# Keeping the high parts of weights in emitted order on ScalarE, in the mixing part of a two-block fp32 model

## The chip, the cores and the metric

The kernel runs on one core of a Trainium2 chip. The metric is the device time of one execution in microseconds (us); the kernel before takes 1950.87 us as the median of three runs, which lie between 1950.57 and 1951.28 us.

## The reference

A sequence of 256 tokens of width 1024 passes through two blocks. The first block has two layers, each with a half-weighted SwiGLU feed-forward, a mixing part, a cross-attention to 256 memory tokens and a second feed-forward. The second block (mLSTM, differential attention, a mixture of 32 experts) is left out here; the change does not reach into it. The mixing part projects the normed tokens to 3328 columns, gives half of the width to an RWKV-7 recurrence and half to a causal attention (MoBA), and projects both back:

```
h = rms_norm(x); p = h @ w_mix_in
# RWKV-7, 8 heads of 64, decay w, rates a, from p through small low-rank products
p = p + (token_shift(p) - p) * mu
state = state * w_t + (state @ -kk_t) b_t^T + v_t k_t^T        # one step per token
y_t = state @ r_t ; y = group_norm(y) + bonus ; y = y * gate
# MoBA: softmax(q k^T + bias) v within one block of 256 tokens, 8 heads
x = x + concat(y, moba) @ w_mix_out
k, v = split(mem @ w_kv)                                       # for the cross-attention that follows
```

All of it is float32.

## The kernel before

**Weights.** All dense weights are a stream of tiles of 128x1024 fp32 in a fixed order. `load` starts the DMA of the next one into a buffer named raw. `parts` (L541) splits one into a high part, `wh`, with an ACTIVATE of ScalarE (a copy rounded to fp32r), and a low part, `wl`, which is raw less wh, with a TENSOR_TENSOR of VectorE. The tokens are split in the same way into XH and XL. A product is then three matmuls (`mm3`): XH with wh, XH with wl, XL with wh. One tile takes 12 matmuls of 128x512. `prefetch` calls `parts` ahead of need, as far as buffers go: in the mixing part there are four raw buffers and two each of wh and wl (`RING`), so the wh of a tile can start only once TensorE is done with the tile two before it. In the feed-forwards other buffers are lent to this ring.

**The mixing part.** `mix` (L884) runs the projections one after the other (`proj`) and starts tasks beside them: `shifted` (token shift), `lora` (the small products), `rwkv_early` for two groups of heads (decays by scans on VectorE, sums that pass through GpSimd), `rwkv_late` with `rwkv_solve` (a 16x16 solve by many small VectorE instructions on a tile W, whose result comes back by DMA into the tiles c and is spread into Y) and `rwkv_chunk` (two chunks of 128 tokens), `moba`, and `xattn_k` (keys and values of the memory for the cross-attention). At its end `add_proj` multiplies by the output weights, which needs all of them.

**What sets the order.** The kernel's own `Weave` chooses which task emits next, by priorities and by a cost model (`Clock`) that says what is due. That gives the order in which instructions are emitted. A scheduler behind it then orders the instructions of each engine anew by when its own model holds them ready; the engine executes them in that order, one behind the other, and waits at the first that is not ready. `tc.keep_in_program_order(z)` adds to z an edge from the instruction emitted just before z on the same engine: z cannot be put ahead of that one. Instructions emitted earlier still may be put behind z.

Every instruction passes through one helper (`TimedEngine`), so all rows of the trace have its line, L378, and are told apart by the names of their tiles. In rows of the order the names carry numbers; the last number of a tile counts emissions.

Of the kernel before, what the change touches and what calls it, by code (L numbers as in the profile page):

```python
# [9 lines left out]
F32 = mybir.dt.float32  # L10
# [3 lines left out]
AF = mybir.ActivationFunctionType  # L14
# [19 lines left out]
class Cols:  # L34


    def __init__(self, *items):
        self.at, self.n = {}, 0
        for name, w in items:
            self.at[name] = (self.n, w)  # L40
            self.n += w
# [46 lines left out]
def stream():  # L88

    out = collections.deque()  # L90

    def put(name, *js):
        out.extend((name, j, i) for j in js for i in range(2))

    ada = iter([("ada", j, i) for j in range(24) for i in range(2)])

    def ffn(name):
        for c in range(NCH):
            for j in range(6):
                if j < 4:  # L100
                    out.append((name, 3 * c + j // 2, j % 2))
                elif c:
                    out.append((name, 3 * c - 1, j % 2))
                if c and (j == 3 or c % 5 == 0 and j == 4):
                    out.append(next(ada))
        put(name, 3 * NCH - 1)

    for l in range(2):
        ffn(f"ffn1{l}")
        put(f"mix{l}", *range(13))  # L110
        put(f"kv{l}", *range(4))
        put(f"mo{l}", *range(4))
        put(f"kv{l}", *range(4, 8))
        put(f"xq{l}", *range(4))
        put(f"xo{l}", *range(4))
        ffn(f"ffn2{l}")
    put("win", *range(14), 14, 15, 16, 17, 18, 19, 20, 21)
    put("br", *range(4))
    put("wo", *range(4))
    for e in range(32):  # L120
        put("exp", 3 * e, 3 * e + 1)
        if e:
            put("exp", 3 * e - 1)
    put("exp", 95)
    return out
# [126 lines left out]
class Clock:  # L252
# [18 lines left out]
    @staticmethod  # L271
    def span(ap):

        (step, parts), *dims = [(int(s), int(n)) for s, n in ap.ap]
        n = math.prod(z for _, z in dims)
        dims = sorted((z for z in dims if z[1] > 1 and z[0]), reverse=True)
        runs, size = [int(ap.offset) % step if step else int(ap.offset)], 1
        while dims and dims[-1][0] <= size:
            s, z = dims.pop()
            size += s * (z - 1)  # L280
        while dims:
            s, z = dims.pop()
            if len(runs) * z > 16:
                size += s * (z - 1)
            else:
                runs = [r + s * i for r in runs for i in range(z)]
        return ap.tensor.name, [(r, r + size) for r in runs], n, parts
# [160 lines left out]
class Prog:  # L448
    def __init__(self, ctx, tc, a):
        self.clock = Clock()  # L450
        self.tc, self.nc, self.a = tc, Timed(tc.nc, self.clock), a
        nc = self.nc
        pool = lambda name, **k: ctx.enter_context(tc.tile_pool(name=name, **k))
        self.cp = pool("cst", bufs=1)
        self.wp = pool("wts", bufs=2)
        self.ap_ = pool("act", bufs=2)
        self.pp = pool("psum", bufs=2, space=PSUM)
        self.dp = pool("dram", bufs=1, space=DRAM)
        self.uid = 0
        self.turn = {}  # L460
        self.weave = Weave(self.clock)
        self.spawn = self.weave.add
        self.order, self.loads, self.ahead = stream(), collections.deque(), collections.deque()
        self.chunks, self.mod = collections.deque(), None
        self.version, self.uses = [1, 1], 0
        self.sp, self.spare = None, {}
        self.behind, self.stop = [], None
        self.loan = {}
        self.tail = self.scaled = None

# [70 lines left out]
    def parts(self, raw):  # L541
        h, l = self.wtile("wh", F32R), self.wtile("wl", F32R)
        with ExitStack() as later:
            for z in self.behind:
                later.enter_context(self.tc.issue_after(z.ins))
            quiet, self.clock.quiet = self.clock.quiet, True
            self.nc.scalar.activation(h, raw, AF.Copy)
            self.nc.vector.tensor_sub(l, raw, h.bitcast(F32))
            self.clock.quiet = quiet
        return h, l  # L550

# [797 lines left out]
    def softmax(self, *parts):  # L1349

        nc = self.nc
        cut = lambda z, n, m: z[:, :n * m].rearrange("p (h k) -> p h k", h=n)
        mx, sm, out = [], [], []
        for dst, src, n, m in parts:
            mx.append(self.k("s8", 8))
            nc.vector.tensor_reduce(mx[-1][:, :n], cut(src, n, m), axis=AX.X, op=OP.max)
            nc.vector.tensor_scalar(mx[-1][:, :n], mx[-1][:, :n], -1.0, None, op0=OP.mult)
        yield 0, -0.5
        for (dst, src, n, m), z in zip(parts, mx):
            v, d = cut(src, n, m), cut(dst, n, m)  # L1360
            sm.append(self.k("s8", 8))
            for h in range(n):
                nc.scalar.activation(d[:, h], v[:, h], AF.Exp, bias=z[:, h:h + 1], accum_out=sm[-1][:, h:h + 1])
            out.append(d)
        yield 0, -0.3
        for (dst, src, n, m), z, d in zip(parts, sm, out):
            ri = self.k("s8", 8)
            nc.vector.reciprocal(ri[:, :n], z[:, :n])
            for h in range(n):
                nc.scalar.activation(d[:, h], d[:, h], AF.Copy, scale=ri[:, h:h + 1])  # L1370
        yield 0, self.due(*out)
        return out
# [1008 lines left out]
    def beyond(self, state, out):  # L2381
# [13 lines left out]
        with self.tc.If(most > P):  # L2395
# [10 lines left out]
            for e in range(8):  # L2406
# [21 lines left out]
             raw=2, wh=2, wl=2)  # L2428


def body(tc, a, out, stage=99):
    with ExitStack() as ctx:
        p = Prog(ctx, tc, a)
        w = p.weave

        def first():
            X = p.next_x(p.vec("gf10"))
            for n in range(min(stage, 8)):
                l, part = divmod(n, 4)
                norm = n == 7 and stage >= 9 and p.spawn(p.final_norm(), 1)  # L2440
                Z = None if n == 7 else p.next_x(p.vec(("gmx", "gxa", "gf2", "gf1")[part] + str((n + 1) // 4)))
                if part == 1:
                    kv = yield from p.mix(l, X)
                elif part == 2:
                    yield from p.xattn(l, X, kv)
                else:

                    p.lend({k: v for k, v in LOAN.items() if n < 7 or k != "raw"})
                    yield from p.ffn(f"ffn{part // 2 + 1}{l}", X)
                    p.lend({})  # L2450
                X = Z
                if norm:
                    yield norm

        with p.work(BUFS):
            p.setup()
            p.spawn(p.setup_later(), 5)
            w.finish(w.add(first(), 10))
            if stage == 9:
                p.settle()  # L2460
        if stage >= 10:
            p.sp = ctx.enter_context(tc.tile_pool(name="second", bufs=1))
            p.spare = SPARE
            with p.work(BUFS2):
                MX = w.finish(w.add(p.block2(), 10))
        if stage >= 11:
            with p.work(BUFS3):
                p.beyond(w.finish(w.add(p.moe(MX, out), 10)), out)
        else:
            for t in range(2):  # L2470
                tc.nc.sync.dma_start(out[t * P:(t + 1) * P], p.x[t])
# [18 lines left out]
```

## Time and profile before

| | us |
|---|---|
| median of three runs | 1950.87 |
| the profiled execution | 1949.61 |
| its span | 1947.6 |
| TensorE (PE) busy | 1897.4 (97%) |
| VectorE (DVE) busy | 1403.1 (72%) |
| ScalarE (ACT) busy | 1059.3 (54%) |
| GpSimd (POOL) busy | 73.3 (4%) |

PE is busy for 97% of the span and idle for 50 us. Of these, 18 us lie in the two mixing parts, one per layer, at 202 to 420 us and, with the same pattern, at 898 to 1116 us; 1.5 us lie in the 478 us between them, and 25 us after them. The mean granted clock over the span is 0.991 of full speed.

### The profile page before, as it was taken

To read this page: it belongs to the slowest core of one execution; us is meant where nothing else is said; L and a number is where in the kernel's file an instruction comes from. 1 tells how busy PE (TensorE), PEld (TensorE's weight loads), DVE (VectorE), ACT (ScalarE), POOL (GpSimd) and SP (SyncE) were. 2 spreads that over 40 slices of the span, in tenths; PEclk is the share of its full clock that TensorE was granted. 3 is DMA by queue.
4 is the path that set the end of the run, shared out by engine and by line. 5 is a ranking of instruction groups with operands and counts; after the bars stand their busy time and mean duration, and the time that the engine had idled before them with its cause. 6 is when DMAs were issued, how large, how long until landed. Compare 5 with 4: busy or idle time off the path is not lost.

```text
span 1947.6 us, 26262 instructions
## 1 busy us (share of the span) xinstructions
PE 1897.4 (97%) x9534; PEld 1532.9 (79%) x9534; DVE 1403.1 (72%) x2287; ACT 1059.3 (54%) x1606; POOL 73.3 (4%) x69
## 2 busy tenths in 40 slices
PE   8999999999999999999999999999999999999997
PEld 6888778888888878888787888888777786877775
DVE  6666787664666676666877655666687677999897
ACT  4444653655544444445536655444555546777674
POOL 0000011000000000000110000000001000000000
PEclk9999999999999999999999999999999999999999
DMA  8766432244566656665314253666564453999996
GB/s 280 249 223 226 128 126 68 86 155 159 172 211 222 216 205 215 220 213 173 134 41 127 97 189 117 222 221 215 183 202 139 150 182 139 337 340 360 332 337 223
DMA packets 114806, 381.41 MB, mean 196 GB/s; under 512 B 17080, under 2 KB 21864, under 8 KB 114544
## 3 DMA queue, kind: packets, MB, share of 16 engines
q1 hardware_dynamic: 114672, 379.68, 58.3%
q8 instruction: 77, 1.26, 0.3%
q14 instruction: 57, 0.47, 0.1%
HBM read 378.03 MB, written 3.17 MB: 196 GB/s over the span
## 4 chain that ended last, share of the span: by engine, by line
PE 76%; issue 11%; DVE 7%; ACT 2%; POOL 1%; DMA 1%; SPq 0%; DVEq 0%; POOLq 0%; ACTq 0%
PE mm L378 40%; PE acc L378 31%; PE tr L378 6%; DVE wl L378 3%; ACT wh L378 1%; POOL rs L378 1%; DVE el L378 1%; DVE s L378 1%; DMA raw<-in_w_dram 1%; DVE XL L378 0%; DVE t1k L378 0%; DVE AR L378 0%; DMA K<-in_mem_dram 0%; DMA x<-in_x_dram 0%; ACT s L378 0%
## 5 line engine op out<-in xcount | busy, mean ns | idle before, releaser
L378 DVE TENSOR_TENSOR wl<-raw,wh 128x1024 fp32r<-128x1024 f32 x648 | 785.2, 1223 | 320.2 <-ACT wh L378 317.2
L378 ACT ACTIVATE wh<-raw 128x1024 fp32r<-128x1024 f32 x648 | 676.3, 1057 | 522.6 <-PE mm L378 295.3
L378 PE MATMUL mm<-wh,XH 128*128 128x512 f32 (+1 forms) x1456 | 579.6, 400 | 3.0 <-ACT s L378 2.4
L378 PE MATMUL mm<-wl,XH 128*128 128x512 f32 (+1 forms) x1456 | 573.5, 394 | 2.6 <-DVE wl L378 2.1
L378 PE MATMUL mm<-wh,XL 128*128 128x512 f32 (+1 forms) x1456 | 571.3, 393 | 0.3
L378 PEld LDWEIGHTS mm<-wl,XH 128*128 128x128 f32 x1456 | 274.4, 188 | 65.7 <-DVE wl L378 10.7
L378 PEld LDWEIGHTS mm<-wh,XH 128*128 128x128 f32 x1456 | 274.7, 189 | 63.5 <-ACT s L378 3.8
L378 PEld LDWEIGHTS mm<-wh,XL 128*128 128x128 f32 x1456 | 274.2, 188 | 57.9 <-DVE XL L378 1.1
L378 PE MATMUL acc<-wh,X 128*128 128x512 f32 x352 | 143.0, 406 | 0.0
L378 PE MATMUL acc<-wh,T 128*128 128x512 f32 x352 | 139.1, 395 | 0.0
L378 PE MATMUL acc<-wl,X 128*128 128x512 f32 x352 | 139.1, 395 | 0.0
L378 PE MATMUL acc<-wl,XH 128*128 128x512 f32 x288 | 115.0, 399 | 2.9 <-DVE wl L378 2.7
L378 PE MATMUL acc<-wh,XH 128*128 128x512 f32 x288 | 114.5, 404 | 0.9 <-ACT XH L378 0.5
L378 PE MATMUL acc<-wh,XL 128*128 128x512 f32 x288 | 114.0, 396 | 0.0
L378 PE MATMUL acc<-wh,ah 128*128 128x512 f32 x256 | 85.7, 396 | 1.3 <-ACT ah L378 1.3
L378 DVE SCALAR_TENSOR_TENSOR el<-raw,vecs,el 128x512 f32<-128x512 f32 x84 | 63.1, 751 | 32.9 <-DMA raw<-in_w_dram 31.1
L378 PEld LDWEIGHTS acc<-wh,T 128*128 128x128 f32 x352 | 66.3, 188 | 15.9
L378 PEld LDWEIGHTS acc<-wl,X 128*128 128x128 f32 x352 | 66.4, 189 | 13.8
L378 PEld LDWEIGHTS acc<-wh,X 128*128 128x128 f32 x352 | 66.3, 188 | 13.4
L378 POOL TENSOR_TENSOR rs<-s,emh 128x2 f32<-128x2 f32 (+2 forms) x28 | 31.6, 1133 | 1147.3 <-DVE s L378 1144.7
L378 PEld LDWEIGHTS acc<-wl,XH 128*128 128x128 f32 x288 | 54.7, 190 | 18.3 <-DVE wl L378 7.5
L378 PEld LDWEIGHTS acc<-wh,XH 128*128 128x128 f32 x288 | 54.4, 190 | 12.5 <-ACT XH L378 1.2
(377 smaller groups left out, 2060.5 us busy)
## 6 DMA issues: line engine op xcount, KB each, us to landing
raw<-in_w_dram SPq DMA_DIRECT2D x696, 512.0 KB
ext<-ext SPq DMA_DIRECT2D x1, 2048.0 KB
K<-in_mem_dram SPq DMA_DIRECT2D x8, 256.0 KB
x<-in_x_dram SPq DMA_DIRECT2D x4, 256.0 KB
bi<-ext SPq DMA_DIRECT2D x4, 256.0 KB
sm<-ext SPq DMA_DIRECT2D x4, 256.0 KB
w<-gates SPq DMA_DIRECT2D x2, 512.0 KB
out_dram<-x SPq DMA_DIRECT2D x4, 256.0 KB
```

The costliest lines, as they stand in the source:

```text
L378: r = f(*args, **kw)
```

## The change

`Prog` gets a flag, `pinned`. It is True while `mix` runs. While it is, `parts` calls `keep_in_program_order` for the ACTIVATE that makes wh; the TENSOR_TENSOR that makes wl is not marked. This holds for every tile split in that time, whichever task asks for it. Nothing is added to or taken from the instructions of any engine.

```diff
@@ Prog.__init__
+        self.pinned = False
@@ Prog.parts
-            self.nc.scalar.activation(h, raw, AF.Copy)
-            self.nc.vector.tensor_sub(l, raw, h.bitcast(F32))
+            made = (self.nc.scalar.activation(h, raw, AF.Copy), self.nc.vector.tensor_sub(l, raw, h.bitcast(F32)))
+            for z in made[:1] if self.pinned else ():
+                self.tc.keep_in_program_order(z)
@@ body, first()
                 if part == 1:
+                    p.pinned = True
                     kv = yield from p.mix(l, X)
+                    p.pinned = False
```

The scheduler's order differs in both mixing parts in the same way. In each layer 17 of about 42 wh come behind work of ScalarE that they preceded, and what depends on them moves on VectorE and TensorE.

The first place is ScalarE in the second group's `rwkv_early` of the first layer, 264 to 290 us in the trace before. t1k, el and COPY t1k are steps of the decay; wh_2485 is the high part of the last tile of MoBA's query projection, wh_2546 that of the first tile of its key projection.

```order
-L378 ACTIVATE wh_2485<-raw_2374 128x1024
-L378 ACTIVATE wh_2546<-raw_2422 128x1024
-L378 ACTIVATE s_596_2604<-mm_2372,rh_1875 128x512
 L378 ACTIVATE t1k_2465<-acc_2459,half_1916 128x256
 L378 ACTIVATE t1k_2469<-acc_2459,half_1916 128x256
@@ -191,15 +186,17 @@
 L378 COPY t1k_2473<-s_561_2456 128x256
 L378 COPY t1k_2475<-s_561_2456 128x256
+L378 ACTIVATE wh_2485<-raw_2374 128x1024
 L378 ACTIVATE t1k_2520<-acc_2460,half_1916 128x256
 L378 ACTIVATE t1k_2528<-acc_2460,half_1916 128x256
```

wh_2485 went from ahead of t1k to behind COPY t1k (with four ACTIVATEs of el in between, which did not move), and wh_2546 further back.

The second place is VectorE at the same time. Y is filled from c, which a DMA brings from the solve; el_2503 is the first scan of the decay (its result is read by COPY pe and AR).

```order
 L378 COPY start<-el_2448 128x8
+L378 TENSOR_TENSOR Y_2221<-c_504_2237,csts 128x512
+L378 MEMSET el_2448 128x8
 L378 COPY pe_2533<-el_2503 128x4
 L378 TENSOR_TENSOR AR_2535<-rkv_1981,el_2503 128x2x128
-L378 MEMSET el_2448 128x8
-L378 COPY pe_2533<-el_2503 128x4
+L378 TENSOR_TENSOR wl_2486<-raw_2374,wh_2485 128x1024
+L378 TENSOR_TENSOR Y_2253<-c_513_2269,csts 128x512
 L378 SCALAR_TENSOR_TENSOR el_2504<-el_2448,start 128x512
```

wl_2486, which stood in the middle of the solve's instructions on W, now stands behind the first Y, which came later, and behind AR.

The third place is ScalarE at the start of the output projection, 400 to 413 us. XH there is the high part of what is multiplied, K keys on their way through TensorE's transposes, wh_3931 a tile of the output weights.

```order
-L378 ACTIVATE wh_3931<-raw_3834 128x1024
 L378 ACTIVATE XH_2150<-t1k_3902 128x2x128
 L378 ACTIVATE K_3893<-tr_3907 128x512
+L378 ACTIVATE XH_2150<-t1k_3916 128x2x128
 L378 ACTIVATE K_3894<-tr_3921 128x512
-L378 ACTIVATE XH_2150<-t1k_3916 128x2x128
+L378 ACTIVATE wh_3931<-raw_3834 128x1024
 L378 ACTIVATE wh_3949<-raw_3873 128x1024
```

wh_3931 went from ahead of two XH and two K to behind all four; its wl on VectorE moved behind the XL in the same way.

## Rows read from the trace of the kernel before

**Rows 1.** Busy time of each engine over the span, from the page.

```profile
PE 1897.4 (97%) x9534; PEld 1532.9 (79%) x9534; DVE 1403.1 (72%) x2287; ACT 1059.3 (54%) x1606; POOL 73.3 (4%) x69
```

**Rows 2.** Groups by line: busy us, mean ns; idle us before, its releaser.

```profile
L378 DVE TENSOR_TENSOR wl<-raw,wh 128x1024 fp32r<-128x1024 f32 x648 | 785.2, 1223 | 320.2 <-ACT wh L378 317.2
L378 ACT ACTIVATE wh<-raw 128x1024 fp32r<-128x1024 f32 x648 | 676.3, 1057 | 522.6 <-PE mm L378 295.3
```

**Rows 3.** Windows: stretch, length, busy of PE, PEld, DVE, ACT, POOL, clock, DMA, GB/s.

```profile
202.00:420.00 218.00, 209.25 (x1396) 171.51 (x1394) 159.01 (x360) 123.21 (x246) 25.07 (x22) 0.98 0.34 106
898.00:1116.00 218.00, 208.65 (x1391) 170.84 (x1390) 158.06 (x354) 122.78 (x246) 24.98 (x22) 0.98 0.32 101
420.00:898.00 478.00, 476.48 (x2167) 388.47 (x2166) 311.28 (x392) 230.18 (x307) 2.09 (x3) 1.00 0.62 204
```

**Rows 4.** Waits, 202 to 420 us: who waits for whom, sum, times, longest.

```profile
ACT wh L378 <- PE mm L378: 22.6, 15, 4.6
```

**Rows 5.** Timeline, first group's rwkv_early: start, us, instruction, idle before it.

```profile
234.76 0.71 ACT L378 COPY t1k<-s 128x256 f32<-128x256 f32 x2 [0.52 <-POOL s L378]
235.87 0.47 PE L378 MATMUL mm<-wh,XH 128*128 128x512 f32 x1
236.17 1.23 DVE L378 TENSOR_TENSOR_SCAN el<-el,start 128x512 f32<-128x512 f32 x1
245.68 1.06 ACT L378 ACTIVATE wh<-raw 128x1024 fp32r<-128x1024 f32 x1 [4.63 <-PE mm L378]
249.56 0.30 PE L378 MATMUL tr<-csts,rkv 128*128 128x128 f32 x1 [1.51 <-DVE rkv L378]
```

**Rows 6.** Timeline, second group's rwkv_early and first solve.

```profile
268.91 2.73 POOL L378 TENSOR_TENSOR s<-s,emh 128x8 f32<-128x8 f32 x1 [20.97 <-DVE s L378]
272.22 1.06 ACT L378 ACTIVATE wh<-raw 128x1024 fp32r<-128x1024 f32 x1 [4.00 <-PE mm L378]
274.17 0.83 ACT L378 ACTIVATE t1k<-acc,half 128x256 f32<-128x256 f32 x2
275.14 0.20 DVE L378 TENSOR_TENSOR W<-W,t1k 32x28 f32<-32x28 f32 x1
276.48 0.70 ACT L378 COPY t1k<-s 128x256 f32<-128x256 f32 x2
276.93 0.74 PE L378 MATMUL tr<-csts,t1k 128*128 128x128 f32 x4 [0.67 <-ACT t1k L378]
277.51 1.27 POOL L378 TENSOR_TENSOR t1k<-csts,pe 128x256 f32<-128x256 f32 x2 [5.87 <-DMA c<-W]
278.22 0.84 DVE L378 TENSOR_TENSOR AR<-rkv,el 128x256 f32<-128x256 f32 x1
278.55 0.50 PE L378 MATMUL mm<-wh,XH 128*128 128x512 f32 x1 [0.88 <-ACT s L378]
280.32 0.67 DVE L378 TENSOR_TENSOR Y<-c,csts 128x512 f32<-128x512 f32 x1
283.24 1.97 PE L378 MATMUL tr<-csts,Y 128*128 128x128 f32 x8 [1.64 <-DVE el L378]
285.04 2.62 PE L378 MATMUL acc<-X,A 128*128 128x128 f32 x16
```

**Rows 7.** Windows in the same stretch.

```profile
279.50:280.00 0.50, 0.50 (x3) 0.40 (x2) 0.50 (x1) 0.00 (x0) 0.00 (x0) 0.50 0.00 0
286.50:287.00 0.50, 0.50 (x7) 0.50 (x6) 0.19 (x1) 0.19 (x1) 0.00 (x0) 1.00 0.64 205
```

**Rows 8.** Timeline, preparation of the memory beside the second chunk.

```profile
352.29 0.59 ACT L378 ACTIVATE T<-acc 128x512 f32<-128x512 f32 x1
353.16 1.00 DVE L378 TENSOR_REDUCE s<-bi 128x2 f32<-128x256 f32 x2
```

**Rows 9.** Timeline, start of the output projection.

```profile
409.92 0.42 ACT L378 ACTIVATE XH<-t1k 128x256 fp32r<-128x256 f32 x1 [0.49 <-DVE t1k L378]
410.26 0.39 PE L378 MATMUL mm<-wh,XH 128*128 128x512 f32 x1
```

**Rows 10.** Timeline, two further idle times of TensorE in the mixing part.

```profile
327.47 0.44 PE L378 MATMUL tr<-csts,YL 128*128 128x128 f32 x2 [1.02 <-DVE YL L378]
346.26 0.63 PE L378 MATMUL tr<-csts,K 128*128 128x128 f32 x4 [0.72 <-DMA K<-in_mem_dram]
```

## The prediction

> **What bounds the kernel now.** The page's busy times come first: PE is busy for 97% of the span, DVE for 72%, ACT for 54% [rows 1]. So TensorE bounds the whole, and a change of order on ACT shows in the time only where it makes PE idle, ends an idle time of PE, or changes the clock that PE is granted. The windows say how much there is to win where the change acts: in the first mixing part PE is busy for 209.25 of 218 us, in the second for 208.65; it idles 8.75 and 9.35 us, against 1.5 us in the 478 us between [rows 3]. The groups show the pair that the change moves: making wh takes 1.06 us, making wl 1.22 us, and before wl DVE has idled 317 us in all for wh [rows 2]. A wh that comes late is thus followed by a wl that comes late, 2.3 us from the start of one to the end of the other. The waits show the other side: in the first mixing part ACT stood with a wh at its head until PE let go of the buffer, 15 times, 22.6 us in all, longest 4.6 us [rows 4]. In that time the ACT work queued behind wh waited as well. The change turns this around: the wh that are moved wait behind ACT work, instead of ACT work behind them. For each place the question is which of the two PE meets first.
>
> PE needs 0.22 us for a matmul (478 us by 2167 in the stretch without gaps [rows 3]), so 2.65 us for the 12 of one tile. Since the same instructions run before and after, I count for each place the idle time of PE that appears less that which goes.
>
> **The change part by part.** Per layer 17 wh move. Most have room: between the end of such a wh and the first matmul on it lay 1.8 to 7.9 us, by my reading of the timeline, and the ACT work put ahead of it is shorter. These cost nothing, as long as PE has the tile before, 2.65 us of work, as cover; a wh without that cover costs up to the 2.3 us above. Four places are left.
>
> *First group's rwkv_early (228 to 250 us).* wh moves behind nine short ACT instructions, of which the last, COPY t1k, waited for POOL and ended at 235.47 [rows 5]. So wh ends at 236.5. Its wl on DVE moves behind the scan that ended at 237.40 [rows 5], and comes to 238.2 with some 0.4 us off for the chain that starts earlier. PE used this tile from 235.87 [rows 5] and can go on with wh alone for two matmuls: about 1.65 us idle, and 0.5 more because the transposes behind it come at a worse moment, +2.1. In return the wait of 1.51 us at 249.56 goes: it was for DVE, which had waited for ACT work behind the wh that stood 4.63 us at ACT's head [rows 5]; a gap of 0.4 us goes as well. Sum 0, from -1.5 (only the gain) to +2 (only the loss).
>
> *Second group's rwkv_early and first solve (264 to 290 us).* Before, the wh at 272.22 stood 4.00 us at ACT's head, t1k came behind it at 274.17, COPY t1k at 276.48, and PE waited 0.67, 0.88 and 1.64 us for this chain: 3.19 us [rows 6]. After, the chain goes ahead. Its COPY waits only for POOL, which ended at 268.91 + 2.73 = 271.64 [rows 6]; I take 271.4, since DVE feeds POOL a little earlier. COPY then ends at 272.1 and wh at 273.2. PE does two matmuls on it, until 273.65, and needs wl. On DVE wl now stands behind the first Y, and Y needs c from the solve's DMA. The solve's last instruction on W ended at 275.34, with two wl of 1.22 us standing in its chain; without them, about 273.5 (some of the room goes to other work). From W's end to c's arrival, which POOL waited for, went 277.51 - 275.34 = 2.17 us [rows 6]. So c is back at 275.7, Y (0.67), two small copies and AR (0.84) follow, and wl runs from 277.2 to 278.4: PE idles 278.4 - 273.65 = 4.75 us. Later the chain acc<-X,A to acc<-Y,T, which had the tile's matmuls beside it, comes earlier (near 283.2, not 285.04 [rows 6]) and with a single matmul between; the copy T between them takes 0.59 us [rows 8], about 0.85 with the hand-overs. Sum 4.75 + 0.85 - 3.19 = +2.4. Bounds: -3.2 if wl is not held (all three waits gone), +5 if Y comes as late as before, since the first Y at 280.32 would put wl two to three us later.
>
> *Memory preparation beside the second chunk (340 to 363 us).* Two wh move behind XH, s, X and T, the last ending at 352.88, and the first wl behind reductions that ended at 354.16 [rows 8]. PE runs the chunk's chain alone, 1.2 us short of wl at its end, and about 0.7 us short at T, where eight matmuls, 1.8 us, lay beside the chain: +1.9. Bounds: 0 (the chunk's end comes earlier by as much) to +3.4 (1.8 of cover gone, and 1.6 for wl).
>
> *Start of the output projection (400 to 413 us).* wh moves behind two XH and two K, its wl behind both XL. The second XH ended at 410.34 [rows 9]; with no wl ahead of its source on DVE it comes about 0.9 us sooner, the K behind it ends at 410.0, wh at 411.05, wl at 412.3. PE was ready for the tile at 410.26 [rows 9]: 0.8 us idle for wh, two matmuls, 0.85 us for wl: +1.65, from 0 to +1.7.
>
> *Absorbed.* Two waits of PE of 1.02 and 0.72 us end with DVE or a DMA [rows 10]. If PE comes later there, these shrink: -0.7, from -1.7 to 0.
>
> *The clock.* From 279.5 to past 286 us PE had a granted clock of 0.50, its lower level of 1.2 GHz, and 1.00 again at 286.5; before the fall stood the waits of 0.67 and 0.88 us, inside it that of 1.64 [rows 6, 7]. My sum supposes one such stretch per layer after, too: its cost is in both times and drops out.
>
> The Trainium skill (TensorE: Matmul & The Clock Gate, HAM oscillation — how this bites in real kernels) says that pauses of TensorE between bursts of matmuls put it back to the lower clock. The trace agrees in that the fall came behind a group of waits, though the pauses here were each under 1 us; by that rule the stall of 4.75 us would bring a fall too, which changes nothing here, and each further stall might, which is the third rival.
>
> **Sum.** 0 + 2.4 + 1.9 + 1.65 - 0.7 = +5.25 us per layer, and both layers move alike: +10.5. The profiled execution took 1949.61 us, its span 1947.6; 1949.61 + 10.5 = 1960.1. It lies 1.26 us below the median of the runs, 1950.87, so the median after is 1961.4; I say 1961. The bounds add up to -6.4 and +12.1 per layer, about -13 and +24 in all.
>
> **The rivals.**
> *Faster: the early chains pay.* The wh at 272.22 and 245.68 no longer stand at ACT's head, and what PE waited for behind them comes early [rows 5, 6]. If c is back by 274 us, wl is not held by Y; then -3.2 and -1.5 at the first two places, and half of the loss at the others, +1.8: -2.9 per layer, 1950.87 - 5.8 = 1945. It decides if PE's wait for the wl behind Y is under 2 us. For it: 22.6 us of such waits of ACT [rows 4]. Against: W's chain and 2.17 us of DMA don't leave room for it.
> *No change.* The edge binds wh to one instruction only, most wh have room, and what is late at one place is taken from PE's idle time at the next, of which there are 8.75 us [rows 3]: 1951. Against: the waits of [rows 10] can take 1.7 us, not 6.
> *Slower still: a second stretch at the lower clock.* If the stalls at 340 to 363 us bring one of 6.8 us more, as 279.5 to 286.3, PE does half of that in it: +3.4 per layer, (5.25 + 3.4) x 2 = 17.3, 1968. For it: a fall behind waits as short as these [rows 6, 7]. Against: the waits of [rows 10] lie at such places too, and the mean clock of the mixing part, 0.98, leaves room for just the one stretch.
>
> **How the numbers follow.** Forecast 0.45, faster 0.24, no change 0.18, slower still 0.13. Within 0.2%, 3.9 us, counts as no change, since that is about what a measurement of this kernel can tell. So faster 0.24, same 0.18, slower 0.58. The range must leave out no more than 0.2: from 1945, which cuts off half of the faster case, to 1969, which holds the third rival but for its tail. The likeliest case by itself has 1955 to 1966.
>
> **What would show it right or wrong.** Right: in the second group's rwkv_early, a wait of PE for wl of 4 to 5 us near 274, in place of those of 0.67, 0.88 and 1.64; on DVE wl directly behind AR; acc<-X,A about 2 us earlier; at the output projection two waits of 0.8 us for wh and wl; PE's idle time in the mixing part near 14 us instead of 8.75. Wrong: c's DMA back before 274.5, so that the wait is under 2 us; a wait of 1.5 us still at 249.56; a second stretch at 0.50, or none, in the clock; or a difference that lies outside the two mixing parts, where I count nothing.

## The result and the profile after

The changed kernel takes 1961.68 us (median of five, 1959.52 to 1965.16), the kernel before on the same chip 1950.57 (1948.84 to 1951.28). The ratio is 1.0056, 95% interval 1.0044 to 1.0069: slower by 8.6 to 13.5 us. The forecast was 1961.

The page of the kernel after: TensorE is busy for 2 us more than before [rows 1] in a span 11.9 us longer, so most of what was added is idle time. Between wl and wh, and between wh and PE, the idle times shift as a change of order would have it [rows 2]: VectorE waits longer for wh, ScalarE less for PE.

```profile
PE 1899.4 (97%) x9534; PEld 1528.9 (78%) x9534; DVE 1404.3 (72%) x2287; ACT 1058.5 (54%) x1606; POOL 70.8 (4%) x69
```

```profile
L378 DVE TENSOR_TENSOR wl<-raw,wh 128x1024 fp32r<-128x1024 f32 x648 | 785.0, 1223 | 334.7 <-ACT wh L378 333.2
L378 ACT ACTIVATE wh<-raw 128x1024 fp32r<-128x1024 f32 x648 | 676.1, 1057 | 507.1 <-PE mm L378 279.6
```

The windows of the two mixing parts, cut at the same points of the work as in [rows 3], and the stretch between them. PE idles 12.98 and 12.26 us in place of 8.75 and 9.35; 478 us between the parts have 1.55 us idle, as before. The forecast had near 14 us of idle time in a part.

```profile
202.69:426.16 223.47, 210.49 (x1396) 170.45 (x1395) 159.30 (x360) 122.91 (x246) 23.57 (x22) 0.98 0.33 103
904.36:1126.43 222.07, 209.81 (x1391) 169.52 (x1390) 157.98 (x354) 122.46 (x246) 23.95 (x22) 0.98 0.31 99
427.00:905.00 478.00, 476.45 (x2165) 388.32 (x2165) 311.34 (x393) 229.20 (x304) 2.09 (x3) 1.00 0.62 203
```

The waits of 202 to 427 us. ACT's wait with a wh at its head [rows 4] went from 22.6 us in 15 times to 14.1 in 8, and PE's wait for wl, 0.2 us before, is now the largest of PE's.

```profile
ACT wh L378 <- PE mm L378: 14.1, 8, 4.3
PE mm L378 <- DVE wl L378: 4.6, 7, 2.2
PE mm L378 <- ACT wh L378: 1.1, 3, 0.4
```

**Lag.** To see where time is lost, the matmuls of two executions are taken each in its own order and compared at the points at which the same amount of work is done (each form weighted with its usual time from one start to the next, 0.227 us for 128x512). The difference in time there is the lag behind before. Differences of the lag are what a stretch costs. Where two executions run their matmuls in different orders the lag depends on the weights: at 264, 300, 962 and 998 us by up to 0.5 us in most runs, in e5, e9 and e11 by up to 2, and in e9 and e11 by up to 1 at 340, 400, 1034 and 1098; at the ends of the mixing parts it does not. In us, at times of the kernel before:

| run | 202 | 264 | 300 | 340 | 400 | 420 | 898 | 962 | 998 | 1034 | 1098 | 1118 |
|---|---|---|---|---|---|---|---|---|---|---|---|---|
| after | 0.7 | 0.9 | 3.1 | 4.2 | 5.1 | 6.2 | 6.4 | 5.9 | 7.9 | 8.4 | 9.4 | 10.4 |
| e1 early tiles only | 0.0 | 0.0 | 1.6 | 2.6 | 2.7 | 2.7 | 2.7 | 2.7 | 5.1 | 5.7 | 6.0 | 6.0 |
| e2 all but these | 0.8 | 1.0 | 2.1 | 1.8 | 2.9 | 4.0 | 4.4 | 3.9 | 5.4 | 5.0 | 5.9 | 6.9 |
| e3 output tile only | 1.0 | 1.0 | 1.2 | 1.2 | 1.3 | 2.4 | 2.5 | 4.1 | 4.4 | 4.4 | 4.4 | 5.6 |
| e5 first tiles only | -0.1 | 0.0 | -2.5 | -1.3 | -2.3 | -2.3 | -1.3 | -1.2 | 1.6 | 1.1 | 1.3 | 1.3 |
| e6 memory tiles only | -0.6 | 1.0 | 1.2 | 1.2 | 2.2 | 2.2 | 2.3 | 2.3 | 1.3 | 1.3 | 2.3 | 2.3 |
| e9 decay behind | -0.1 | -0.1 | -7.0 | -6.6 | -3.0 | -4.5 | -3.5 | -3.5 | -10.6 | -10.6 | -6.2 | -7.6 |
| e11 e9 with pins | 0.5 | 0.7 | -6.1 | -2.1 | 4.9 | 3.7 | 3.7 | 3.2 | -3.5 | -2.4 | 6.4 | 5.4 |

Of the 12.07 us between the two profiled executions, 5.48 came in the first mixing part, 4.07 in the second, 0.7 ahead of the first and 1.8 elsewhere. The last two are not the change's, since the engines' orders differ only at 209 to 412 and 902 to 1108 us of before: what comes ahead of 202 us differs by -0.6 to 1.0 between the runs, and 0.8 us of what comes behind stand at a stretch at the granted clock 0.50 in the second block, which lasts 10.2 us here (1417.9 to 1428.2) and 6.8 in before (1409.3 to 1416.1).

**Second group's rwkv_early and first solve.** The rows of the kernel after that answer to [rows 6], ScalarE first:

```profile
273.02 0.92 ACT L378 ACTIVATE t1k<-acc,half 128x256 f32<-128x256 f32 x2 [4.76 <-DVE W L378]
275.44 0.70 ACT L378 COPY t1k<-s 128x256 f32<-128x256 f32 x2
276.04 1.06 ACT L378 ACTIVATE wh<-raw 128x1024 fp32r<-128x1024 f32 x1
...
272.69 0.24 DVE L378 TENSOR_TENSOR W<-W,t1k 32x88 f32<-32x88 f32 x1
277.36 1.14 DVE L378 TENSOR_TENSOR Y<-c,csts 128x512 f32<-128x512 f32 x1
278.50 0.41 DVE L378 TENSOR_TENSOR AR<-rkv,el 128x256 f32<-128x256 f32 x1
278.83 1.21 DVE L378 TENSOR_TENSOR wl<-raw,wh 128x1024 fp32r<-128x1024 f32 x1
...
275.88 0.85 PE L378 MATMUL tr<-csts,t1k 128*128 128x128 f32 x4 [2.80 <-ACT t1k L378]
277.15 0.73 PE L378 MATMUL mm<-wh,XH 128*128 128x512 f32 x2 [0.41 <-ACT wh L378]
280.10 0.80 PE L378 MATMUL mm<-wl,XH 128*128 128x512 f32 x1 [2.22 <-DVE wl L378]
285.52 1.95 PE L378 MATMUL acc<-X,A 128*128 128x128 f32 x16
```

PE waits 2.80, 0.41 and 2.22 us, with 0.27 us at 270.49 in all 5.70, in place of 3.19. acc<-X,A was forecast 2 us earlier and came 0.5 us later. wl stands behind Y and AR as the order showed. But the first and largest wait is for ScalarE: its t1k, no longer behind a wh, still started only at 273.02, because it waited for a VectorE instruction on W, the one that ended at 272.93.

**The clock.** The stretch at 0.50 (1.2 GHz) lies at 277.9 to 284.7, before at 279.5 to 286.3: as long, and one per layer, as the forecast supposed.

```profile
277.50:278.00 0.50, 0.38 (x2) 0.00 (x0) 0.50 (x1) 0.31 (x1) 0.45 (x1) 0.88 0.20 23
284.50:285.00 0.50, 0.50 (x4) 0.37 (x3) 0.50 (x3) 0.44 (x1) 0.00 (x0) 0.79 0.00 0
```

**The other places**, PE's waits of the kernel after. At the first group [rows 5] the wait of 1.51 us fell to 0.48; at the memory's preparation [rows 8] there are waits of 0.69 us for T and 0.42 for wl; at the output projection [rows 9] 0.28 and 0.52.

```profile
239.22 0.50 PE L378 MATMUL mm<-wl,XH 128*128 128x512 f32 x1 [0.69 <-DVE wl L378]
249.88 0.30 PE L378 MATMUL tr<-csts,rkv 128*128 128x128 f32 x1 [0.48 <-DVE rkv L378]
331.22 0.44 PE L378 MATMUL tr<-csts,YL 128*128 128x128 f32 x2 [0.93 <-DVE YL L378]
355.39 2.05 PE L378 MATMUL acc<-Y,T 128*128 128x128 f32 x16 [0.69 <-ACT T L378]
358.33 0.50 PE L378 MATMUL mm<-wl,XH 128*128 128x512 f32 x1 [0.42 <-DVE wl L378]
415.48 0.74 PE L378 MATMUL mm<-wh,XH 128*128 128x512 f32 x2 [0.28 <-ACT wh L378]
416.74 0.50 PE L378 MATMUL mm<-wl,XH 128*128 128x512 f32 x1 [0.52 <-DVE wl L378]
```

### The profile page after: what moved, and what is told of

Read it like the earlier page. It is cut to its first block, busy times and chain, and to the rows that moved or that the text cites. A ratio compares the mean times of both kernels' runs of the same rounds, so it can differ in the third digit from the quotient of the medians.

```text
span 1959.5 us, 26267 instructions
## 1 busy us (share of the span) xinstructions
PE 1899.4 (97%) x9534; PEld 1528.9 (78%) x9534; DVE 1404.3 (72%) x2287; ACT 1058.5 (54%) x1606; POOL 70.8 (4%) x69
## 4 chain that ended last, share of the span: by engine, by line
PE 73%; issue 12%; DVE 9%; ACT 2%; DMA 2%; POOL 1%; SPq 0%; DVEq 0%; POOLq 0%; ACTq 0%
PE mm L378 38%; PE acc L378 30%; PE tr L378 5%; DVE wl L378 4%; DMA raw<-in_w_dram 1%; ACT wh L378 1%; DVE s L378 1%; POOL rs L378 1%; DVE XL L378 1%; DVE t1k L378 1%; DVE W L378 0%; DVE el L378 0%; DVE AR L378 0%; DMA K<-in_mem_dram 0%; DMA x<-in_x_dram 0%
## 5 line engine op out<-in xcount | busy, mean ns | idle before, releaser
L378 POOL TENSOR_TENSOR rs<-s,emh 128x2 f32<-128x2 f32 (+2 forms) x28 | 28.9, 1034 | 1149.1 <-DVE s L378 1147.7
L378 ACT ACTIVATE t1k<-mm,rh 128x256 f32<-128x256 f32 x80 | 37.9, 473 | 49.0 <-PE mm L378 49.0
```

Source lines behind the costliest of these rows:

```text
L378: r = f(*args, **kw)
```

## The experiments

Theory A: each place costs by itself what PE waits there for tiles that come late, and the places add. The rivals are named with the runs. Each ratio is to runs of the kernel before taken beside that run; their medians were 1950.43 to 1951.76 us.

**e1 and e2: the second group's tiles alone, and all the others.** One set of tiles is pinned, or left free:

```diff
+PIN = {("mix", 8, 1), ("mix", 9, 0), ("mix", 9, 1), ("mix", 10, 0)}
-            for z in made[:1] if self.pinned else ():
+            for z in made[:1] if self.pinned and self.unit in PIN else ():       # e2: not in PIN
```

> Keeps in order only four tiles of each mixing part: those of the second group's rwkv_early and first solve (last tile of MoBA's queries, first two of its keys, and the next). Theory A, each place costs by itself what TensorE waits there for wl and wh that come late: in the first mixing part a lag of 2.2 us against before at 300 us, as in the changed kernel, about 1 more in the chunk behind it, nothing at the other places; both layers 4 to 6 us, about 1955.5. Theory B, one place's loss is swallowed by TensorE's idle time later in the part, and only many places together lose: lag at the end of the part under 1 us, total within 2 us of before.

> The changed kernel with those same four tiles left free. Theory A: the waits of 2.80, 0.41 and 2.22 us near 275 are gone and those of before (0.67, 0.88, 1.64) are back; the rest of the loss stays, some 2 to 3 us per layer: about 1956. Theory B (the loss is not local): the time stays near 1961, or falls back to 1951.

e1: 1956.59 us, ratio 1.0028 (1.0018 to 1.0038); e2: 1957.27, 1.0037 (1.0025 to 1.0050). By the lag e1 costs 2.7 and 3.2 us in the two layers, e2 3.2 and 2.5; the sums 5.8 and 5.7 stand against 5.5 and 4.1 of the change. Theory A holds in the first layer within 0.4 us, and in the second the parts together cost 1.6 us less than apart. Theory B falls: either part by itself loses. But the places are not cleanly apart: in e2, whose four tiles were free, PE's waits of before did not come back at their size; 0.66, 1.24 and 2.50 us stand where before had 0.67, 0.88 and 1.64, and the lag rises by 1.1 us there in the first layer and 1.5 in the second.

**e3 and e6: the output projection's tile, and the memory's two.** The same edit with `("mo", 0, 1)`, or with `("kv", 0, 1), ("kv", 1, 0)`.

> Keeps in order only the second tile of the output weights, in each layer. Theory A: two waits of about 0.7 us each for wh and wl at 412 us and nothing else: 1.1 us per layer, 2.2 in all, about 1953. Theory B: no difference at the end of the part.

> Keeps in order only two tiles of each mixing part, the second and third of the memory's projection (340 to 363 us). Theory A: TensorE waits near 355 us, lag 1.7 us there, of which about half is given back by 390 (in the changed kernel the lag rose from 4.16 to 6.78 and fell to 5.08): 0.9 us per layer, 1.8 in all. The forecast on record had 1.9 per layer, 3.8 in all. Theory B, it is all given back by the idle times behind: lag 0 at 400 us.

e3: 1955.49 us, 1.0014 (1.0004 to 1.0023). The lag rises by 1.2 us at the output projection in each layer, as expected. The rest of this execution's difference is no part of that: 1.6 us at 898 to 962 came with a stretch at the granted clock 0.50, at 950.1 to 953.5, which the kernel before does not have there, and 2 us lie in the second block. e6: 1954.01, 1.0013 (1.0003 to 1.0023). The lag rises by 1.0 us in each layer between 340 and 400 (1034 and 1098), half of what the forecast had; 1.6 us at 202 to 264, where this kernel's order is that of before, came with a stretch at 0.50 at 250.6 to 254.0 (the last section shows it).

**e5 and e10: the first group's tiles, in both layers and in one.** `("mix", 4, 1), ("mix", 5, 0), ("mix", 5, 1), ("mix", 6, 0)`; e10 with "mix0" alone.

> Keeps in order only four tiles of each mixing part that are split during the first group's rwkv_early (228 to 250 us). Theory A: TensorE loses about 2 us near 237 for a late wl and gets about 2 back at 249.56, where its wait of 1.51 us shrinks: the lag behind before is between -0.6 and +0.3 us at 264 us and stays there, time within 1.5 us of before. Theory B, the late wl is not paid back: lag of 2 us at 264 in each layer, total 4 more.

e5: 1949.61 us, 0.9992 (0.9983 to 1.0002). At 264 us the lag is 0.0, so the late wl is paid back, as theory A has it. What then came was not expected: from start to end of the mixing part the first layer gains 2.2 us, and the second loses 2.5. In the second, PE's waits near 975 us grew from 3.1 to 4.9 us. In the first, the scheduler had put one more wl (276.75) ahead of the decay's first scan (279.01) on VectorE:

```profile
273.45 1.23 DVE L378 TENSOR_TENSOR wl<-raw,wh 128x1024 fp32r<-128x1024 f32 x1 [0.30 <-ACT wh L378]
276.75 1.23 DVE L378 TENSOR_TENSOR wl<-raw,wh 128x1024 fp32r<-128x1024 f32 x1 [0.76 <-ACT wh L378]
279.01 1.22 DVE L378 TENSOR_TENSOR_SCAN el<-el,start 128x512 f32<-128x512 f32 x1
```

> Keeps in order the four tiles near the first group's rwkv_early in the first layer alone. In the run with both layers the first gained 2.3 us, because there wl of the last key tile came ahead of the second group's decay chain, and the second lost 2.5. Theory A: the first layer's gain stands by itself, 2.3 us, about 1949. Theory D, that gain was an accident of that execution: within 0.5 us of before at 420 us.

e10: 1948.93 us, 0.9991 (0.9983 to 1.0000). The lag falls by 2.4 us in the first layer once more, so that gain comes with the order and not with one execution; in time it stands at the edge of what the runs can tell. In both runs the stretch at 0.50 there lasts 3.4 us in place of 6.8, and how much of the gain is the clock is not shown.

**e4: what held t1k.** The solve's scratch comes from another ring of buffers:

```diff
-            z = self.k("t1k", 256)[:n, :2 * j * (15 - j)]...
+            z = self.k("X", 512)[:n, :2 * j * (15 - j)]...
```

> The changed kernel, with the scratch tiles of the 16x16 solve taken from the ring X instead of the ring t1k that the decay's t1k tiles use too. Theory A, the decay chain on ScalarE started only at 273 us because its t1k tile takes the buffer of the solve's tenth step: now t1k starts by 270.5 us and COPY t1k ends by 273, TensorE's wait of 2.80 us before the transposes of t1k falls under 1 us; the solve and the decay then share VectorE, so that wl of the next tile comes late instead, 3 to 6 us: total 1959 to 1965. Theory B, t1k waits for something else of the solve: it still starts at 273 and the wait of 2.80 stays, total as the changed kernel.

e4: 1965.59 us, 1.0074 (1.0057 to 1.0091). t1k started at 269.58, behind PE and no longer behind W, and the wait of 2.80 us is gone: the ring of four buffers had tied the decay to the solve. Theory A holds, though the time lies just above its 1965. The time did not fall, since VectorE then has solve and decay in one line ahead of the tiles: PE waits 2.15, 1.57 and 2.42 us instead.

```profile
269.58 0.84 ACT L378 ACTIVATE t1k<-acc,half 128x256 f32<-128x256 f32 x2 [1.31 <-PE acc L378]
...
272.87 0.60 PE L378 MATMUL tr<-csts,t1k 128*128 128x128 f32 x4
276.57 0.50 PE L378 MATMUL mm<-wl,XH 128*128 128x512 f32 x1 [2.15 <-DVE wl L378]
280.70 1.10 PE L378 MATMUL mm<-wh,XH 128*128 128x512 f32 x2 [1.57 <-ACT wh L378]
284.22 1.09 PE L378 MATMUL tr<-csts,Y 128*128 128x128 f32 x4 [2.42 <-DVE Y L378]
```

**e7 and e8: a third pair of wh and wl.** The kernel before, with two free buffers lent in the first part of `mix` (`self.lend(dict(wh=["gr"], wl=["pt"]))`), given back ahead of the key or the query projection.

> The kernel before (nothing kept in order) with a third pair of wh and wl in the first part of the mixing part: the buffers gr and pt are lent until the key projection begins. Theory A: wh and wl then no longer stand at the head of ScalarE and VectorE for a buffer, TensorE's idle times near 240 to 250 (2.4 us) and 277 to 283 us (3.2 us) shrink by a half or more: 2 to 3 us less per layer, about 1946. Theory C: VectorE, on which the solve, the decay and every wl run in one line, sets that stretch, and a third pair changes nothing there: within 2 us of before.

> As the run with the third pair, but lent only until the query projection begins. Theory A: the idle times near 240 to 250 shrink as there, those near 277 to 283 do not: 1 to 1.5 us less per layer, about 1948. Theory C: within 2 us of before.

Both were wrong: 1966.72 us, 1.0075 (1.0059 to 1.0092), and 1961.23, 1.0049 (1.0032 to 1.0066). In e7 the lag is some -6 us at 340 us and +10.4 at 420: tiles ran ahead, and were then missing beside the chunks and the attention, where PE waits 4.58 us for a wl at 348.85.

**e9: the reverse edge.** No wh is pinned. The decay of the second group is emitted once the second key tile is split, and put behind its wh and wl (parts left out are marked):

```diff
+        nxt = (f"mix{l}", 9, 1)
+        if g == 1:
+            yield lambda: nxt in self.low                     # low[u] = (wh, wl), kept by prefetch
 ...
         zw, za = self.ps("acc"), self.ps("acc")
 ...
+            with self.tc.issue_after(self.low[nxt][0].ins) if g == 1 else nullcontext():
                 act(th, B(zw, b), AF.Tanh, bias=col(half, 0, b), scale=0.5)
 ...
+            with self.tc.issue_after(self.low[nxt][1].ins) if g == 1 else nullcontext():
                 nc.vector.tensor_copy(st(self.start), st(z))
```

> The kernel before (no wh kept in order), with the reverse edge at one place: the second group's decay chain (t1k on ScalarE, the first scan's start on VectorE) is put behind wh and wl of the last key tile but two, so that three tiles stand ahead of it. Theory A, the order that wins is the one in which tiles come ahead of the chain, since TensorE then has work while the chain runs: its waits of 0.67, 0.88 and 1.64 us near 277 to 283 shrink below 1.5 in sum, lag 2 to 4 us ahead of before in each layer behind the first chunk: 1943 to 1947. Theory C, VectorE's line sets that stretch in any order: the chain comes later by as much as tiles come earlier, within 2 us of before.

e9: 1942.50 us, 0.9964 (0.9951 to 0.9976), faster than both. In place of PE's waits of 0.67, 0.88 and 1.64 us stand 0.80 and 0.12, and no stretch at the lower clock is left: the mixing part has a mean clock of 1.00 in place of 0.98.

```profile
202.00:415.50 213.50, 206.14 (x1395) 169.63 (x1394) 157.01 (x360) 122.65 (x246) 22.93 (x22) 1.00 0.33 108
278.00:284.00 6.00, 5.07 (x35) 4.12 (x34) 5.90 (x13) 4.47 (x7) 0.00 (x0) 1.00 0.30 94
```

The lag falls by some 7 us in each layer up to the first chunk, and 2 to 3 of these are given back behind it: the tiles done early are missing as cover there. The window says what the gain is made of: the first mixing part is 4.5 us shorter than in [rows 3], of which 3.1 us are busy time (206.14 in place of 209.25 us for the same matmuls) and 1.4 idle time. The 6.8 us at 0.50 in before hold 5.2 us of work of PE (1.64 are a wait), which at full speed would take 2.6. By this count more than half of the gain is the clock that no longer falls, which the expectation had not reckoned with.

**e11 and e12: e9 with every wh pinned, and e9 for both groups.**

> The changed kernel (every wh of the mixing part kept in order) with the decay chain put behind wh and wl of the second key tile as in the run before. Theory A, the changed kernel loses in the second group's stretch because there the chain is emitted ahead of the tiles and the edge then keeps the tiles behind it: with the chain emitted later the edge costs nothing there, TensorE's waits of 2.80 and 2.22 us near 275 are gone, and what stays is the other places, about 2 us per layer: 1945 to 1948. Theory B, keeping wh in order costs 5 us per layer wherever the chain stands: 1951 to 1954.

> The kernel with the second group's decay chain behind the second key tile, and the first group's chain put behind the first tile of the third projection's pair in the same way. Theory A in its plain form (tiles ahead of the chain always win): TensorE's 3.1 us of waits near 232 to 250 shrink by half, 1 to 1.5 us per layer, about 1940. Rival: at the first group TensorE has tiles enough already (its waits come from the transposes behind), and the later chain delays the solve: no gain or up to 2 us lost per layer, 1942 to 1947.

e11: 1955.90 us, 1.0025 (1.0015 to 1.0034); e12: 1958.35, 1.0039 (1.0024 to 1.0053). Both expectations of the time were too low. In e11 the second group's stretch is much as in e9 (lag -6.1 at 300 us, one wait of 0.35 us), so the edge costs nothing there when the chain is emitted behind the tiles; but all of that and more is lost between 320 and 366 us, where PE waits for a tile's wh and wl and then, with no tile beside it, for the second solve, and where the clock now falls. The waits of PE there:

```profile
334.56 0.73 PE L378 MATMUL mm<-wh,XH 128*128 128x512 f32 x2 [1.00 <-ACT wh L378]
336.34 0.50 PE L378 MATMUL mm<-wl,XH 128*128 128x512 f32 x1 [1.05 <-DVE wl L378]
345.79 1.09 PE L378 MATMUL tr<-csts,Y 128*128 128x128 f32 x4 [2.68 <-DVE Y L378]
```

The window of that stretch, with the clock after POOL's busy time:

```profile
345.00:365.00 20.00, 18.93 (x130) 16.76 (x132) 13.49 (x29) 13.35 (x37) 1.83 (x3) 0.83 0.17 54
```

In e12 the loss lies in the same stretch, with waits of 1.56 us at 341.39 and 4.73 at 352.18 (its traced execution, 1963.87 us, was the slowest of its five). The clock is not most of e11's loss: of the 9.8 us by which its lag rises from 300 to 420, the 6.8 us at 0.50 (345.1 to 351.9) can cost 3.4 at the most; in the second layer the fall lasts 3.4 us, and the lag rises by 8.9 all the same. So places do not add where one makes PE run ahead: what a pin costs depends on how much work stands beside the next chain.

## Why the prediction was right

The time (1961 against 1961.68) and the sum (10.5 us against 9.55 in the two mixing parts) came out as forecast, and the mechanism was right in the main: tiles that come late make PE idle. The steps fit less well than their sum, per layer:

| step | forecast | first layer | second layer |
|---|---|---|---|
| first group's rwkv_early | 0 | +0.2 | -0.5 |
| second group's, first solve | +2.4 | +2.2 | +2.0 |
| first chunk behind it (as "absorbed") | -0.7 | +1.1 | +0.5 |
| memory preparation, attention | +1.9 | +0.9 | +0.9 |
| output projection | +1.65 | +1.1 | +1.1 |

That the sum fits is in part luck: the first chunk cost 1.8 and 1.2 us more than forecast, memory and output together 1.5 us less in each layer. And the traced executions differ by 12.07 us, of which 2.5 lie outside the mixing parts and are not the change's.

*First group:* a loss near 238 us (lag 2.9) paid back at 249.56, shown by the change's rows and by e5.

*Second group:* the size was right and half of the reason wrong, since the forecast had COPY t1k wait for POOL alone. The forecast had COPY t1k end at 272.1 us and laid the whole wait of 4.75 us on wl behind Y and AR. COPY ended at 276.14: t1k waited for its buffer, which the eleventh of the solve's fourteen steps gives back (32x88, ended at 272.93); in before that wait was hidden behind the 4.00 us for the wh [rows 6], and e4 shows it (the expectation of e4 has tenth for eleventh). The same step in before ended at 272.63, ahead of the end of that wh:

```profile
272.39 0.24 DVE L378 TENSOR_TENSOR W<-W,t1k 32x88 f32<-32x88 f32 x1
```

So 3.21 us of waits go to that, and 2.22 to wl, of which 1.7 (from wh's end at 277.10 to wl's start at 278.83) are Y and AR. The size came out right all the same, since both lead to the same line on VectorE: e4, with the first wait taken away, ends no earlier. The 0.85 us for the copy T did not come: acc<-X,A was not earlier, and PE has no idle time between it and acc<-Y,T.

*Absorbed* was wrong in sign. The wait of 1.02 us [rows 10] did not shrink: 0.21 and 0.93 stand in its place (and 0.61 for that of 0.72). The tile whose wl was made at 291 us in before got it at 316, so that the chunk had one tile less beside it. e1, which pins that tile among others, shows the same rise, 1.1 and 0.6 us; e2, which leaves it free, -0.3 and -0.5.

*Memory preparation* was over-sized: 0.69 us for T as reckoned, but 0.42 for wl, not 1.2. *Output projection*: 0.80 us of waits, not 1.65. wh began at 414.37, which less the lag of 5.08 us is 409.3, not 410.0, and the waits were 0.28 and 0.52 for 0.8 and 0.85.

*The signs.* wl directly behind AR and the idle time of the part came as named. The wait for wl was 2.22 us and not 4 to 5, acc<-X,A was not earlier, and the two waits at the output projection were under 0.8.

*The rivals.* The early chains did not pay, as the forecast had it, but the price named against them (W and the DMA of c) was not all of it. The sign that was to decide, a wait for the wl behind Y of under 2 us, does not: in the second layer that wait is 1.79 us, and the place still costs 2.0, since 2.82 us for t1k stand ahead of it. The second stretch at the lower clock did not come in the change; it came in e11. The Trainium skill (TensorE: Matmul & The Clock Gate, HAM oscillation — how this bites in real kernels) has TensorE's pauses between bursts of matmuls bring the lower clock, where each pause is longer than the burst. The traces agree in that every such stretch in the mixing parts stands behind waits and that e9, without those near 277 to 283 us, has none there; they differ in that the fall in before came behind gaps of only 0.67 and 0.88 us.

The second layer loses 1.4 us less than the first with the same order. Of this, 0.7 come ahead of the four places, at a tile near 211 and 911 us that the forecast did not count: in the second layer before had two waits there, in the first only one of 0.13 us, and after has one of about 0.5 us in both (in the table this stands in the first row). The second layer of before:

```profile
911.16 0.73 PE L378 MATMUL acc<-wh,XH 128*128 128x512 f32 x2 [0.40 <-ACT wh L378]
912.42 0.50 PE L378 MATMUL acc<-wl,XH 128*128 128x512 f32 x1 [0.53 <-DVE wl L378]
```

The other half, most of it in the first chunk, stays open, and so does how e11's loss divides among its waits.

## What to carry to other kernels

Where the engine that bounds a kernel is fed tile by tile, look for each tile that is moved behind a chain whether a tile's worth of work stands in front of that chain: with it the moves here cost nothing that the lag shows, without it part of the tile's making was paid, 0.80 us of waits at the output projection and 2.22 for the wl behind the solve. The better order here was the reverse one, tiles ahead of the chain, made where the chain is emitted, and more than half of its gain was the clock; in e11 the edges on every wh took the cover away elsewhere. Before reckoning with a chain that comes earlier, follow the buffers of its ring: a wait at the head of a queue can hide another one behind it.

## What the runs showed of the hardware that was not expected

The stretch at the lower clock is not bound to the order: e6, with the order of before at 264 to 290 us, had it at 284.7 to 288.1 us and full speed at 279.5. The windows, and then PE's row behind them:

```profile
279.50:280.00 0.50, 0.40 (x2) 0.36 (x3) 0.50 (x1) 0.50 (x2) 0.32 (x1) 1.00 0.21 24
284.50:285.00 0.50, 0.50 (x5) 0.50 (x4) 0.50 (x3) 0.00 (x0) 0.00 (x0) 0.72 0.00 0
288.00:288.50 0.50, 0.50 (x6) 0.50 (x5) 0.50 (x1) 0.44 (x1) 0.00 (x0) 0.87 0.02 8
```

```profile
284.29 1.60 PE L378 MATMUL tr<-csts,Y 128*128 128x128 f32 x8 [2.58 <-DVE el L378]
```

It did not gain by that: its transposes of Y began at 284.29, which less its lag of 1.04 is 283.25, as in [rows 6], after a wait of 2.58 us for VectorE in place of 1.64. At this place the half clock ahead of a wait cost nothing.

It can also come or stay away with the same order and the same waits. The wait of 1.51 us at 249.56 in before [rows 5] is followed by full speed. In e6, whose order differs from before only behind 338 us, the same wait (248.99) is followed by 3.4 us at 0.50, and the lag rises by 1.6 us; e3 has the same in the second layer. A row of PE and a window of e6, then the same window of before:

```profile
248.99 0.30 PE L378 MATMUL tr<-csts,rkv 128*128 128x128 f32 x1 [1.51 <-DVE rkv L378]
253.50:254.00 0.50, 0.50 (x5) 0.50 (x4) 0.00 (x0) 0.50 (x1) 0.00 (x0) 0.50 0.04 4
```

```profile
253.50:254.00 0.50, 0.50 (x3) 0.42 (x3) 0.49 (x2) 0.50 (x2) 0.00 (x0) 1.00 0.09 15
```

So of two traces that differ by some 2 us the clock in their rows is to be compared before the order is blamed.
